# One plan of the order of issue over three stages of an encoder step, in place of three plans

## The chip, the core and the metric

The kernel runs on one core of one Trainium2 chip. The metric is the device time of one execution, in microseconds (us). PE is TensorE (matmul), PEld its weight load, DVE VectorE, ACT ScalarE, POOL GpSimd, and SP the engine whose queue issues every DMA of this kernel.

## The reference, cut to what matters

One layer of a streaming encoder, for a prompt of 2048 rows and a sample of 32 rows that share the weights (width 1024, all float32). Each sub-layer is normalised before and after and added to the residual.

```python
hp = rmsnorm(xp, g_pre_mix)
qa, ka, va, qb, kb, vb, la, r = mix_inputs(hp, w_in, w_alpha2, b_alpha)   # one projection, 3088 columns
oa = chunk_band_prompt(qa, ka, va, rel_bias)         # 8 heads x 64: own 64-row chunk and the 8 before it
ob, sp = gla_recurrence(qb, kb, vb, la, s0, block)   # 4 heads, key 64, value 128, gated, causal
xp = xp + rmsnorm(mix_output(oa, ob, r, g_gla_out, w_o), g_post_mix)

mk, mv = mem_kv(mem_prompt, g_mem, w_mk, w_mv)       # 256 memory rows
xp = xp + rmsnorm(mem_attention(rmsnorm(xp, g_pre_mem), mk, mv, w_mq, w_mo), g_post_mem)   # 4 heads x 256

xp = xp + rmsnorm(swiglu(rmsnorm(xp, g_pre_ffn), w_gate, w_up, w_down), g_post_ffn)        # hidden 2816
# the 32 sample rows go the same way, against cached keys, values and state
```

## The kernel before, in words

Every large product is made from three products of a high and a low part (`split`: ACT rounds a copy, L386, and DVE or POOL subtracts, L390; `mm3` issues the three). `mm3` and some others issue through the helper `led` (L383). The trace shows all these at L383, L386 and L390 whatever calls them, so its rows are told apart by their tiles.

**Stage A** (mixing) takes blocks of 512, 512, 512 and 544 rows. `proj` makes queries, keys, values and gates and puts them in DRAM; `attn` makes band attention (`band_group`: scores `s`, softmax, transposes `pt`, values `po`, L750 and L755) and the gated attention (`gla_mix`: small products `g_s` of 64x64, L922 and L926); `out_proj` makes the output projection (`wops`), a norm (`sqa`), the residual `y` (L1053, L1054; x0r is loaded at L1052 and x1d stored at L1055), a second norm (`sqb`, L1026, L1027, L1033) and the scaled input of stage B (L1061), which is stored in DRAM as `h1d` (L1062). Stage A's last block of `out_proj` comes after all its attention. Stage A also makes the memory's keys and values (`mkd`, `mvd`) and block 0's queries for stage B.

**Stage B** (cross-attention) takes five blocks of 416 rows. `load_kv` loads the memory's keys and values (`kr` L1186, `vr` L1190) and splits them into `kTp` and `vTp`; `mem_h` loads h1d of a block and splits it into `m`; `mem_q` makes queries (`mqps`); `mem_attn` makes scores (`ms`), softmax, transposes (`mpt`) and values (`mpv`, into `mo`); `mem_out` makes the output projection (`mops`) into tiles `y`, and `mem_fin` two norms (`norm_fm`: squares at L402 and L405, sums `n_acc` at L406, a product with ones `n_ps` at L408), the residual (L1304, L1305) and the input of stage C (L1309), stored as `h2d` (L1310). The y tiles of odd blocks (1 and 3) and of even ones lie in different pools. Blocks overlap: while block b's heads run, block b + 1's queries are made, and for the last block the output projection of the one before.

**Stage C** (feed-forward) takes three blocks of 696, 692 and 692 rows, each as two column halves with a Strassen-like scheme of seven products: `ffn_raw` loads h2d into four `hr` tiles (L1367), `ffn_ops` forms seven split operands `mf` from their sums and differences (subtractions at L1352), `unit_w` does the same for weights, `unit` issues products `pg` and `pu`, and `down` the products `pdn`.

Each stage opens pools of on-chip memory of its own and closes them at its end, so a pool of stage B lies over memory that pools of stage A had, and a pool of stage C over pools of stage B and over the weight pool that A and B share. An instruction that first writes such memory waits for the old users; the framework adds these waits.

The order in which each engine issues is planned when the kernel is built. `Order._read` walks the traced instructions and takes each one's duration from a formula (`_cost`), the instructions it must follow (through the tiles that both touch) and the tiles it uses. `_pass` then plays the stage: engines that take the ready instruction with the least due time, tiles that hold one of their tag's buffers from the first use to the last. `queue` makes a first order from the program's own priorities, then three times a backward pass, which gives due times, and a forward pass with them; of the four orders it keeps the one that ends first and writes it down as edges from each instruction to the next of its engine. It was called at the end of each stage, and read only what was traced since the call before:

```python
        traced = self.block.bb.instructions
        at = 0
        if self.last is not None:
            at = next(k for k in reversed(range(len(traced))) if traced[k] is self.last) + 1
        self.last = traced[-1]
        self._read(traced[at:])
```

So each stage's plan began with all engines idle, all its memory free and all its inputs there, and ended where its last instruction did. No edge stood between the chain of one stage and that of the next; how the chains are merged on an engine was left to the framework's scheduler.

Of the kernel before, what the change touches and what calls it, by code (L numbers as in the profile page):

```python
# [17 lines left out]
P = 128  # L18
# [28 lines left out]
class Order:  # L47
# [3 lines left out]

    ENGINES = ("PE", "Activation", "DVE", "Pool", "SP")
    SLOW = 1.1
    PASSES = 3

    def __init__(self, tc):
        self.tc = tc
        self.block = tc.nc.cur_bb  # L60
        self.last = None
        self.edge = mybir.DependencyInfo(mybir.DependencyClass.NoSync, mybir.DependencyReason.DATA)

    @staticmethod
# [6 lines left out]
    def _cost(self, ins, kind, eng, outs, inps):  # L71

        n = self._free(outs[0])
        slow = self.SLOW
        if eng == "PE":
            if any(a.tensor.name.startswith(("ident", "anti")) for a in inps):
                return (max(30.0, n * 0.86) if n < 128 else 110.0), 250.0
            if any(a.dtype == F32 for a in inps):
                if n <= 64 and list(inps[0].ap)[0][1] <= 64:
                    return 45.0, 300.0  # L80
                return 2 * max(n * 0.84, 60.0 if n < 128 else 108.0), 300.0
            t = n * 0.4385 + 6.5
            return (max(t, 111.0 if n >= 128 else 60.0) if n < 256 else t), 250.0
        if eng == "SP":
            return 450.0, 2200.0
        if kind == "InstMemset":
            t = 60 + n * 0.5
        elif eng == "Activation":
            if kind == "InstActivation":
                t = 170 + n * 0.9 + (195 if len(outs) > 1 else 0)  # L90
            else:
                t = 165 + n * (0.87 if outs[0].dtype == F32R else 0.82)
        elif eng == "Pool":
            t = 170 + n * 2.35
        elif kind == "InstTensorCopy":
            t = 150 + n * 1.05
        elif kind == "InstTensorTensor":
            t = 200 + n * 1.15
        elif kind == "InstTensorReduce":
            m = self._free(inps[0])  # L100
            t = 60 + m * (1.95 if m > 2 * n else 1.0)
        elif kind == "InstReciprocal":
            t = 130 + n * 6.4
        elif kind == "InstTensorScalarPtr":
            t = 120 + n * 0.83 if len(inps) < 3 else (230 + n * 1.75 if n > 256 else 200 + n * 1.4)
        else:
            t = 245 + n * 1.05
        return t * slow, 90.0

    @staticmethod  # L110
    def _cells(ap):
# [22 lines left out]
        p0 = ap.offset // row  # L134
        return p0, p0 + pat[0][1], bits

    def _read(self, traced):

        self.ops, self.eng, self.dur, self.lat, self.size, self.prio = [], [], [], [], [], []
        self.pred, self.uses, tile_of = [], [], {}  # L140
        self.tiles = []
        log = []
        for ins in traced:
            kind = type(ins).__name__
            eng = str(ins.engine).split(".")[-1]
            if kind in ("BassTilePoolBoundary", "InstLoadActFuncSet") or eng not in self.ENGINES:
                continue
            outs = [a.bass_ap for a in ins.outs if hasattr(a, "bass_ap")]
            inps = [a.bass_ap for a in ins.ins if hasattr(a, "bass_ap")]
            i = len(self.ops)  # L150
            d, l = self._cost(ins, kind, eng, outs, inps)
            size = 4.0
            for _, c in outs[0].ap:
                size *= c
            pred, use = set(), []
            for aps, wr in ((inps, False), (outs, True)):
                for ap in aps:
                    t = ap.tensor
                    if type(t).__name__ != "Tile":
                        continue  # L160
                    k = tile_of.get(t.name)
                    if k is None:
                        k = tile_of[t.name] = len(self.tiles)
                        self.tiles.append(t)
                        log.append([])
                    if t.space == PSUM:
                        p0, p1, bits, wr_ = 0, P, 1, True
                    else:
                        p0, p1, bits = self._cells(ap)
                        wr_ = wr  # L170
                    keep = []
                    for e in log[k]:
                        j, w, q0, q1, b = e
                        if j != i and (wr_ or w) and q0 < p1 and p0 < q1 and b & bits:
                            pred.add(j)
                        if not (wr_ and j != i and p0 <= q0 and q1 <= p1 and not b & ~bits):
                            keep.append(e)
                    keep.append((i, wr_, p0, p1, bits))
                    log[k] = keep
                    if t.space != DRAM and k not in use:  # L180
                        use.append(k)
            self.ops.append(ins)
            self.eng.append(self.ENGINES.index(eng))
            self.dur.append(d)
            self.lat.append(l)
            self.size.append(size)
            self.prio.append(ins.bass_priority)
            self.pred.append(sorted(pred))
            self.uses.append(use)
        n = len(self.ops)  # L190
        self.succ = [[] for _ in range(n)]
        for i in range(n):
# [14 lines left out]
    def _pass(self, prio, back=None):  # L207
# [21 lines left out]
        parked = {g: [] for g in turn}  # L229
        rest = self.count[:]  # L230
        held = [False] * len(self.tiles)
        ready = [[] for _ in self.ENGINES]
        idle = [True] * len(self.ENGINES)
        start, end = [0.0] * n, [0.0] * n
        events = []
        moved = 0.0
# [78 lines left out]
        return start, end  # L315

    def queue(self):
        traced = self.block.bb.instructions
        at = 0
        if self.last is not None:  # L320
            at = next(k for k in reversed(range(len(traced))) if traced[k] is self.last) + 1
        self.last = traced[-1]
        self._read(traced[at:])
        n = len(self.ops)
        best = None
        prio = self.prio
        for turn in range(self.PASSES + 1):
            start, end = self._pass(prio)
            if best is None or max(end) < best[0]:
                best = (max(end), start)  # L330
            if turn == self.PASSES:
                break
            back, fin = self._pass([-(s + d) for s, d in zip(start, self.dur)], back=end)
            whole = max(fin)
            prio = [whole - b for b in fin]
        start = best[1]
        tail = {}
        for i in sorted(range(n), key=lambda i: (start[i], i)):
            e = self.eng[i]
            if e in tail:  # L340
                self.tc.add_manual_dep(self.ops[i], self.ops[tail[e]].name, self.edge, reason="order of issue")
            tail[e] = i
        return best[0]


@with_exitstack
def encoder_step(ctx, tc, ins, outs):
# [8 lines left out]
    dpool = ctx.enter_context(tc.tile_pool(name="dpool", bufs=1, space=DRAM))  # L356
    RW = dict(reuse_waits="tile")

    order = Order(tc)
    PRI = 4000  # L360
    QLEAD = 0.5
    ident = cpool.tile([P, P], F32, name="ident")
# [793 lines left out]
        o1, o2, fin = out_proj(NB - 1)  # L1156
        merge(o1 + o2 + fin)

    order.queue()


    lo_set[0] = [POOL, DVE]
    dense_lead[0] = 0
    with ExitStack() as ph:
# [150 lines left out]
        for b in range(len(CB)):  # L1315
# [7 lines left out]
            if b != len(CB) - 2:  # L1323
                for it in out:
                    it()

    order.queue()


    wph.close()  # L1330
# [280 lines left out]
                down(gs, us, (0,), dn)  # L1611
                finish_rows(0, xts)

    order.queue()


_INS = ["x_prompt", "x_sample", "mem_prompt", "cache_a_k", "cache_a_v", "state_gla", "cache_mem_k", "cache_mem_v",
# [49 lines left out]
```

## Time and profile before

| | |
|---|---|
| time, median of 3 runs | 3460.98 us (3458.7 to 3461.36) |
| profiled execution | 3458.72 us, its span 3456.9 us |
| mean granted TensorE clock | 0.971 |
| instructions | 60285 |
| DMA | 488.57 MB, mean 141 GB/s |

The span is the time from the first to the last instruction on the core; the time of an execution is a little longer. A stretch such as 1920:1990 is in us from the span's start. An arrow in a row reads "waited for": `[14.49 <-ACT vTp L386]` is 14.49 us of idle time before this instruction that ended when ACT had written vTp. In rows of a line or tile the three numbers are the shortest, the median and the longest duration in ns.

### The profile page before, as it was taken

What the parts mean: (1) busy time and instruction counts of PE and PEld (TensorE: products, weight loads), DVE (VectorE), ACT (ScalarE), POOL (GpSimd) and SP (SyncE); (2) the same over time, 40 slices, a digit from 0 to 9 for tenths busy, and PEclk for the clock granted to TensorE, in tenths of its full rate; (3) what the DMA queues carried; (4) which work ended last, traced back from release to release, by engine and by line L of the source; (5) the groups of instructions that cost most, each with busy time, mean ns of one, the idle gap of its engine ahead of it and who ended that gap; (6) DMA issues with size and microseconds to landing.
All of it is one profiled execution on the core that took longest, in us unless ns stands there. A gap on an engine that the chain in (4) does not pass through costs nothing.

```text
span 3456.9 us, 60285 instructions
## 1 busy us (share of the span) xinstructions
PE 3282.8 (95%) x22211; PEld 3095.9 (90%) x22211; DVE 2395.7 (69%) x4395; ACT 1692.9 (49%) x3730; POOL 1352.5 (39%) x1086
## 2 busy tenths in 40 slices
PE   7999999999999899799999599999899998999998
PEld 6888988999977778799999499999799998899998
DVE  5477777666567887657776776667876667876665
ACT  5455555655455556456655343334443433533334
POOL 3243232132255425434542543334353334543332
PEclk9999999999999999899999699999899999999999
DMA  9765754665356637566653532222242222322223
GB/s 280 247 194 158 231 172 132 192 186 158 114 166 207 207 119 233 170 190 195 186 175 110 191 114 74 74 74 74 87 135 74 74 78 86 104 81 74 74 74 91
DMA packets 550045, 488.57 MB, mean 141 GB/s; under 512 B 48488, under 2 KB 496801, under 8 KB 549749
## 3 DMA queue, kind: packets, MB, share of 16 engines
q1 hardware_dynamic: 549749, 484.71, 46.2%
q8 instruction: 175, 2.87, 0.3%
q14 instruction: 121, 0.99, 0.1%
HBM read 369.68 MB, written 114.91 MB: 140 GB/s over the span
## 4 chain that ended last, share of the span: by engine, by line
PE 49%; DVE 4%; issue 2%; ACT 1%; DMA 1%; POOL 1%; SPq 0%; DVEq 0%; POOLq 0%; ACTq 0%
PE pdn L383 14%; PE pg_X L383 7%; PE pu_X L383 7%; PE mops L383 5%; PE pg_Y L383 3%; PE pu_Y L383 3%; PE mqps L383 2%; PE pg_Z L383 2%; PE pu_Z L383 2%; PE mpv L383 1%; PE ms L383 1%; DVE y L1304 1%; DVE hr L1352 0%; DVE acc L1535 0%; DVE mf L390 0%
## 5 line engine op out<-in xcount | busy, mean ns | idle before, releaser
L383 PE MATMUL pdn<-u,wd 128*128 128x346 f32 (+1 forms) x3168 | 521.9, 323 | 27.8 <-DVE acc L1355 25.5
L383 PEld LDWEIGHTS pdn<-u,wd 128*128 128x128 f32 x3168 | 508.9, 190 | 30.5 <-DVE acc L1355 26.6
L386 ACT CAST wg_s<-wg_r 128x512 fp32r<-128x512 f32 x231 | 139.8, 620 | 405.6 <-DVE wg_r L1352 180.5
L1355 DVE TENSOR_TENSOR acc<-acc,pdn 128x346 f32<-128x346 f32 (+1 forms) x464 | 234.9, 513 | 116.5 <-PE pdn L383 114.4
L390 POOL TENSOR_TENSOR wu_s<-wu_r,wu_s 128x512 fp32r<-128x512 f32 x132 | 192.1, 1465 | 250.9 <-ACT wu_s L386 245.1
L383 PE MATMUL pg_X<-mf,wg_s 128*128 128x346 f32 (+1 forms) x1584 | 282.6, 326 | 1.6 <-DVE mf L390 1.0
L383 PE MATMUL pu_X<-mf,wu_s 128*128 128x346 f32 (+1 forms) x1584 | 276.5, 322 | 0.0
L390 POOL TENSOR_TENSOR wg_s<-wg_r,wg_s 128x512 fp32r<-128x512 f32 x99 | 136.4, 1379 | 329.8 <-ACT wg_s L386 329.8
L383 PEld LDWEIGHTS pg_X<-mf,wg_s 128*128 128x128 f32 x1584 | 259.8, 192 | 3.7 <-ACT mf L386 1.8
L383 PEld LDWEIGHTS pu_X<-mf,wu_s 128*128 128x128 f32 x1584 | 255.7, 189 | 0.3 <-POOL wu_s L390 0.3
L383 PE MATMUL wvr_ps<-wvr_s,mv 128*128 128x256 f32 (+3 forms) x1632 | 225.4, 287 | 0.0
L383 PE MATMUL wops<-om,wo_s 128*128 128x512 f32 (+1 forms) x960 | 206.8, 360 | 2.1 <-DVE y L383 1.3
L383 PEld LDWEIGHTS wvr_ps<-wvr_s,mv 128*128 128x128 f32 (+1 forms) x1632 | 203.6, 183 | 4.3 <-issue 1.5
L383 PE MATMUL mops<-mo,wmo_s 128*128 128x416 f32 x960 | 191.1, 354 | 0.0
L390 POOL TENSOR_TENSOR u<-sg,u 128x346 fp32r<-128x346 f32 (+1 forms) x132 | 141.0, 1078 | 116.6 <-ACT u L386 116.6
L386 ACT CAST wu_s<-wu_r 128x512 fp32r<-128x512 f32 x231 | 134.3, 619 | 101.9 <-DVE wu_r L1352 69.2
L383 PEld LDWEIGHTS mops<-mo,wmo_s 128*128 128x128 f32 x960 | 178.2, 188 | 3.7 <-issue 1.1
L383 PEld LDWEIGHTS wops<-om,wo_s 128*128 128x128 f32 x960 | 152.8, 189 | 26.5 <-issue 2.3
L383 PE MATMUL mqps<-m,wmq_s 128*128 128x416 f32 x768 | 169.2, 363 | 5.2 <-DVE m L390 5.2
L750 PE MATMUL po<-prt,v 128*128 128x128 f32 x1120 | 169.6, 278 | 0.0
L750 PEld LDWEIGHTS po<-prt,v 128*128 128x128 f32 x1120 | 153.0, 193 | 5.3 <-issue 0.6
L383 PE MATMUL pg_Y<-mf,wg_s 128*128 128x346 f32 (+1 forms) x792 | 142.2, 328 | 14.4 <-ACT mf L386 8.3
(410 smaller groups left out, 7942.6 us busy)
## 6 DMA issues: line engine op xcount, KB each, us to landing
wg_r<-in_w_ffn_gate_dram SPq DMA_DIRECT2D x66, 512.0 KB, 4.8
wu_r<-in_w_ffn_up_dram SPq DMA_DIRECT2D x66, 512.0 KB, 3.8
wd_r<-in_w_ffn_down_dram SPq DMA_DIRECT2D x66, 512.0 KB, 3.5
wmq_r<-in_w_mq_dram SPq DMA_DIRECT2D x80, 256.0 KB, 3.1
wmo_r<-in_w_mo_dram SPq DMA_DIRECT2D x80, 256.0 KB, 3.0
wo_r<-in_w_o_dram SPq DMA_DIRECT2D x64, 256.0 KB, 3.2
ks<-kad SPq DMA_DIRECT2D x28, 512.0 KB, 5.5
wvr_r<-in_w_in_dram SPq DMA_DIRECT2D x48, 256.0 KB, 4.0
```

What stands on the lines that cost most here:

```text
L383: return f(*a, **k)
L386: ACT.copy(hi, src)
L390: lo_eng.tensor_tensor(out=lo, in0=src, in1=hi.bitcast(F32), op=ALU.subtract)
L750: PE.matmul(po[:, e * P : e * P + n], lhsT=v[:kk, j, :], rhs=prt[:kk, j, :n], start=j == 0, stop=j == len(rows) - 1)
L1304: DVE.scalar_tensor_tensor(out=y[k], in0=y[k], scalar=gains["g_post_mem"][:, k : k + 1], in1=r, op0=ALU.mult, op1=ALU.mult)
L1355: eng.tensor_tensor(out=out, in0=a, in1=b, op=ALU.add)
```

## The change

`queue` is called once, after stage C, and reads all instructions of the program. `_read` notes where pools are opened and closed. For a pool that lies over memory of closed pools it adds a gate to the plan: a step on no engine, of no duration, that follows every instruction that used those pools, and that every instruction that uses the new pool follows. The three calls at the stages' ends become one. The estimate for a float32 product with up to 64 rows of output per partition and up to 64 partitions of input goes from 45 to 82 ns; in this kernel that is `g_s` and its like. The gates are in the plan alone: they are no instructions, and no waits are added to the program by them.

```diff
     ENGINES = ("PE", "Activation", "DVE", "Pool", "SP")
+    GATE = 5
...
                 if n <= 64 and list(inps[0].ap)[0][1] <= 64:
-                    return 45.0, 300.0
+                    return 82.0, 300.0
...
+        opened, closed, owner = {}, {}, {}
+        for p in self.tc.info.pools:
+            if p.space != DRAM:
+                size = sum(m.bufs * (-(-m.max_size_bytes // P // 32) * 32) for m in dict(p.tag_meta).values())
+                opened[p.alloc_inst.name] = (p.id, p.space, size)
...
+        stack, gone, gate, inside = {}, {}, {}, {}
         for ins in traced:
...
+            if ins.name in opened:
+                p, space, size = opened[ins.name]
+                lo = max([q[2] for q in stack.values() if q[0] == space], default=0)
+                stack[p] = (space, lo, lo + size)
+                before = [q for q, (s, a, b) in gone.items() if s == space and a < lo + size and lo < b]
+                if before:
+                    gate[p] = len(self.ops)
+                    self._add(None, self.GATE, (0.0, 0.0), 0.0, 0, sorted({i for q in before for i in inside.get(q, ())}), [])
+            elif ins.name in closed:
+                space, lo, hi = stack.pop(closed[ins.name])
+                gone = {q: v for q, v in gone.items() if not (v[0] == space and lo <= v[1] and v[2] <= hi)}
+                gone[closed[ins.name]] = (space, lo, hi)
...
                     if t.space != DRAM and k not in use:
                         use.append(k)
+                        p = owner.get(t.name)
+                        inside.setdefault(p, []).append(i)
+                        if p in gate:
+                            pred.add(gate[p])
...
     def queue(self):
-        traced = self.block.bb.instructions
-        at = 0
-        if self.last is not None:
-            at = next(k for k in reversed(range(len(traced))) if traced[k] is self.last) + 1
-        self.last = traced[-1]
-        self._read(traced[at:])
+        self._read(self.block.bb.instructions)
...
             e = self.eng[i]
+            if e == self.GATE:
+                continue
             if e in tail:
                 self.tc.add_manual_dep(self.ops[i], self.ops[tail[e]].name, self.edge, reason="order of issue")
...
-    order.queue()          # at the end of stage A
...
-    order.queue()          # at the end of stage B
...
-    order.queue()          # at the end of stage C
+    issue_order.queue()
```

More of the change, by code (lines that the diff above doesn't have):

```diff
@@ L60, in __init__ @@
         self.block = tc.nc.cur_bb
-        self.last = None
         self.edge = mybir.DependencyInfo(mybir.DependencyClass.NoSync, mybir.DependencyReason.DATA)
@@ L135, in _cells, with _add @@
         return p0, p0 + pat[0][1], bits
+    def _add(self, ins, eng, cost, size, prio, pred, use):
+        self.ops.append(ins)
+        self.eng.append(eng)
+        self.dur.append(cost[0])
+        self.lat.append(cost[1])
+        self.size.append(size)
+        self.prio.append(prio)
+        self.pred.append(pred)
+        self.uses.append(use)
     def _read(self, traced):
@@ L142, in _read @@
         log = []
+        opened, closed, owner = {}, {}, {}
[3 more added lines that the diff above has]
+                opened[p.alloc_inst.name] = (p.id, p.space, size)
+                if p.release_inst is not None:
+                    closed[p.release_inst.name] = p.id
+                for t in p.alloc_inst.bass_pool_tiles or ():
+                    owner[t.name] = p.id
+        stack, gone, gate, inside = {}, {}, {}, {}
         for ins in traced:
@@ L150, in _read @@
             i = len(self.ops)
-            d, l = self._cost(ins, kind, eng, outs, inps)
             size = 4.0
@@ L181, in _read @@
                         use.append(k)
[L182 to L189, printed above, removed]
+                        p = owner.get(t.name)
+                        inside.setdefault(p, []).append(i)
+                        if p in gate:
+                            pred.add(gate[p])
+            self._add(ins, self.ENGINES.index(eng), self._cost(ins, kind, eng, outs, inps), size, ins.bass_priority, sorted(pred), use)
         n = len(self.ops)
@@ L231, in _pass @@
         held = [False] * len(self.tiles)
-        ready = [[] for _ in self.ENGINES]
-        idle = [True] * len(self.ENGINES)
+        ready = [[] for _ in range(self.GATE + 1)]
+        idle = [True] * len(ready)
         start, end = [0.0] * n, [0.0] * n
@@ L342, in queue @@
             tail[e] = i
-        return best[0]
 @with_exitstack
@@ L357, in encoder_step @@
     RW = dict(reuse_waits="tile")
-    order = Order(tc)
+    issue_order = Order(tc)
     PRI = 4000
```

## The prediction

> **What bounds the kernel now.** I read the page first: busy times, then the slices.
>
> ```profile
> span 3456.9 us, 60285 instructions
> PE 3282.8 (95%) x22211; PEld 3095.9 (90%) x22211; DVE 2395.7 (69%) x4395; ACT 1692.9 (49%) x3730; POOL 1352.5 (39%) x1086
> PE   7999999999999899799999599999899998999998
> PEclk9999999999999999899999699999899999999999
> ```
>
> TensorE is the bound: 95% busy. Its row of tenths dips at few places, and at the deepest one, slice 23 of 40, the granted clock falls to 0.6 as well. With so little slack on average, the question is what the dips are worth. The second view is the table of stretches, cut at the dips (columns: length, then busy us and count of PE, PEld, DVE, ACT, POOL, then the granted clock):
>
> ```profile
> 100.00:950.00 850.00, 848.98 (x7036) 776.17 (x7036) 588.42 (x1442) 460.09 (x1130) 237.47 (x216) 1.00 0.59 178
> 1000.00:1400.00 400.00, 374.46 (x2662) 319.44 (x2661) 310.10 (x624) 228.89 (x554) 186.67 (x147) 0.96 0.62 190
> 1430.00:1480.00 50.00, 24.55 (x98) 21.08 (x97) 36.09 (x48) 18.46 (x42) 21.27 (x12) 0.62 0.62 193
> 1600.00:1900.00 300.00, 297.56 (x1724) 284.30 (x1723) 200.62 (x359) 176.11 (x410) 126.55 (x92) 1.00 0.53 161
> 1920.00:1990.00 70.00, 27.62 (x102) 22.18 (x101) 50.98 (x52) 24.11 (x35) 29.12 (x18) 0.59 0.56 181
> 2400.00:2520.00 120.00, 99.80 (x594) 94.83 (x593) 103.72 (x129) 57.45 (x99) 59.19 (x42) 0.91 0.29 90
> 2520.00:2890.00 370.00, 370.00 (x2334) 370.00 (x2333) 246.52 (x388) 145.63 (x286) 151.14 (x120) 1.00 0.29 87
> 2890.00:3000.00 110.00, 91.03 (x537) 87.25 (x536) 92.99 (x115) 53.48 (x91) 49.06 (x34) 0.91 0.29 87
> ```
>
> Inside the stages PE does not stop: idle 1.0 of 850 us in the first half of stage A, 2.4 of 300 in stage B, 0.0 of 370 in stage C. Where stages meet it does. Busy time flatters these stretches, since a matmul at half clock counts double, so I price them by count. Stage B's pace is 1724/300 = 5.75 matmuls per us, so the 98 of 1430:1480 are worth 17.0 us and **33.0 us are lost between A and B**. Stage C's pace is 2334/370 = 6.31, so the 102 of 1920:1990 are worth 16.2 us and **53.8 us are lost between B and C**. The two turns inside stage C, from one block of 692 or 696 rows to the next, lose 120 - 594/6.31 = 25.9 and 110 - 537/6.31 = 24.9 us by the same rule; the end of A (1000:1400) idles 25.5 us. Only the first two, 86.8 us together, are places where one plan ended and another began.
>
> What ends them, first from A to B: PE and the DMA queue in order of time, and the row of the last attention products of A.
>
> ```profile
> 1441.62 1.06 PE L383 MATMUL mqps<-m,wmq_s 128*128 128x416 f32 x2 [5.17 <-DVE m L390]
> 1457.47 2.18 PE L1033 MATMUL sqb_ps<-acc,ones 128*128 128x272 f32 x4 [4.50 <-DVE acc L1027]
> 1474.14 1.06 PE L383 MATMUL mpv<-prR,vTp 128*128 128x416 f32 x2 [14.49 <-ACT vTp L386]
> 1450.36 5.96 SPq L1055 DMA_DIRECT2D x1d<-y  x3
> 1461.76 5.19 SPq L1062 DMA_DIRECT2D h1d<-y  x8
> 1469.11 0.51 SPq L1190 DMA_DIRECT2D vr<-mvd  x1
> L755 DVE COPY o<-po x8: 260/288/295, 1328.2 to 1361.2; 64x128 f32<-64x128 f32 x8
> L383 PE MATMUL mqps<-m,wmq_s 128*128 128x416 f32 x76 | 20.2, 406 | 5.2 <-DVE m L390 5.2
> 1517.14 36.41 PE mops L383 x192
> ```
>
> PE waits 14.5 us for vTp, whose load was issued at 1469, behind A's eleven stores of x1d and h1d, though attention, whose memory vTp takes, had ended at 1361. Meanwhile only 76 of the 192 query products (mqps) of block 1 had been issued (that row is of the stretch 1417:1453); the other 116, which need nothing of A's last chain, are worth 116 x 36.41/192 = 22 us.
>
> From B to C, PE, then SP, ACT and DVE:
>
> ```profile
> 1904.82 19.31 PE L383 MATMUL mops<-mo,wmo_s 128*128 128x416 f32 x101
> 1955.37 1.75 PE L408 MATMUL n_ps<-n_acc,ones 128*128 128x416 f32 x2 [26.95 <-POOL n_acc L406]
> 1971.25 0.66 PE L383 MATMUL pg_Y<-mf,wg_s 128*128 128x348 f32 x1 [8.33 <-ACT mf L386]
> 1924.20 0.37 SPq L1367 DMA_DIRECT2D hr<-h2d  x1
> hr<-h2d SPq DMA_DIRECT2D x2, 696.0 KB, 7.6
> 1956.31 1.35 ACT L386 CAST mf<-hr 128x1392 fp32r<-128x1392 f32 x1 [2.61 <-DMA h2d<-y]
> 1959.83 8.47 DVE L1309 SCALAR_TENSOR_TENSOR y<-y,g_pre_ffn,n_r 128x416 f32<-128x416 f32 x8
> L390 DVE TENSOR_TENSOR mf<-hr,mf x15: 1586/1600/2687, 1957.7 to 2924.3; 128x1384 fp32r<-128x1384 f32 x10, 128x1392 fp32r<-128x1392 f32 x5
> L1352 DVE TENSOR_TENSOR hr<-hr,hr x12: 1586/1602/2687, 1968.2 to 2921.3; 128x1384 f32<-128x1384 f32 x8, 128x1392 f32<-128x1392 f32 x4
> L1309 DVE SCALAR_TENSOR_TENSOR y<-y,g_pre_ffn,n_r 128x416 f32<-128x416 f32 x16 | 14.2, 936 | 1.8 <-ACT n_r L395 1.8
> ```
>
> The last product of B ends at 1924. C's first input (hr) is issued at that moment and lands about 7.6 us later, at 1932. But its first cast, into mf, starts at 1956: it waited for a store of h2d out of block 3's y tiles, whose memory mf takes over. Then DVE runs eight scalings of block 4 (8.47 us) before it goes on with C's operands.
>
> **The change part by part.** No instruction of the computation is added or removed; the planner runs at build time and costs the chip nothing. The three plans (three chains of order edges on each engine, merged by the framework) become one chain on each engine. So the whole effect is which instruction stands behind which, on PE, ACT, DVE, POOL and the SP queue.
>
> *A to B.* One plan sees that vTp's memory is free after attention and that mpv needs it, so the vr loads (4) can stand ahead of the 16 stores of x1d and h1d in SP's queue, and the splits that follow them likewise. The 14.5 us go. What is late next is mo, which lies over A's working tiles and so waits for the sqb chain, to about 1460; under it lie the 22 us of query products. Against a full recovery: DVE is busy 36.1 of the 50 us, most of it A's own residual, and 5.2 + 4.5 us of the waits are for DVE. I keep 14 of the 33.0 us as lost: **-19 us**. Bounds: 0 (DVE keeps the order slow) and -33.
>
> *B to C.* A plan of B alone has no reason to finish block 3's h2 early; now a gate says that C's operand memory hangs on it. With it done under the last 19.3 us and more of mops products, the first cast can start at 1932, the landing, instead of 1956: 24 us. Then seven operands are built by 9 DVE instructions of 1.6 us beside two on POOL: 9 x 1.6 = 14.4 us, and each operand feeds 12 products of gate and 12 of up, 24/6.31 = 3.8 us, more than the 14.4/7 = 2.1 us that DVE takes for one. So PE loses the 8 us to landing, the first split (1.35 + 1.6 = 3 us), about half of the next 13 us, and some 5 us because block 4's h2 (14.2 us of DVE for 16 such scalings in this stretch) must still be done before C's accumulators get their memory: 8 + 3 + 6 + 5 = 22 us lost in place of 53.8. **-32 us**. Bounds: -10 (only the eight scalings move out of the way, 8.47 us and a little) and -43 (11 us stay, landing and first split).
>
> The clock falls to 0.59 in this stretch. [...]
>
> Stores and loads that move in SP's queue: if a load that is ready gets behind a store that is not, everything behind it waits. Both plans have that risk; I cost it at nothing, covered by the weights that lie loaded ahead, and if the cover fails, at about one wait as now seen, 14.5 us.
>
> *The corrected estimate* (45 to 82 ns) is for the 64x64 products of the gated attention:
>
> ```profile
> L926 PE MATMUL g_s<-g_W x1536: 218/218/367, 216.2 to 1285.3; 64*64 64x64 f32 x192
> L926 PE MATMUL g_s<-g_kq x256: 218/218/311, 217.9 to 1285.5; 64*64 64x64 f32 x128
> L922 PE MATMUL g_s<-g_W x128: 218/267/367, 216.2 to 1284.6; 64*64 64x64 f32 x128
> 222.53 0.27 PE L922 MATMUL g_s<-g_W 64*64 64x64 f32 x1
> 223.60 0.33 PE L800 MATMUL pt<-ident,u_sb 128*128 128x128 f32 x1
> ```
>
> The code issues 15 products for each of 4 heads and 16 tiles, 960; the trace has 1920 records, two for one. One head's 30 records (the first and what follows the last are shown) take 223.60 - 222.53 = 1.07 us, 71 ns for a product: 82 is nearer than 45. The plan of A was 960 x 37 ns = 35.5 us short of PE time. What better numbers bring is bounded by A's idle time: 1.0 us in its first half, 25.5 us at its end. I take 0, with -20 and +20 as bounds: a new order there can as well open a gap.
>
> *Stage C.* Its steady part has no idle time and its turns were in one plan before: 0, bounds -5 and +10. If the order puts C's first Silu between B's last Ln and Exp, ScalarE reloads its table, 1.28 us each, on an engine busy 24.11 of 70 us there: hidden.
>
> ```profile
> L1459 ACT ACT_TABLE_LOAD x5 | 6.4, 1283 | 0.1
> ```
>
> The sum: -19 - 32 + 0 + 0 = -51 us against this execution's own 3458.7 (span 3456.9 and 1.8 around it): 3408. The runs' median is 3461.0, 2.3 above it, so **3410**.
>
> **The rivals.**
>
> *The seams stay full of VectorE.* PE's holes close only where order was the cause; DVE is the engine with work in both seams (36.1 of 50 and 51.0 of 70 us), and its work is only rearranged. For: the waits on m, acc and the eight scalings. Against: the 14.5 and 24 us waits were for a load and a store, and DVE has 13.9 and 19.0 us of these stretches idle. Then about 10 us at each seam: 3461 - 20 = 3441.
>
> *Slower: one pass for three stages.* The planner makes four orders and keeps the one with the shortest total; before, each stage kept its own best of four. If the order kept is not A's best, A pays over its whole length, since on an in-order engine one late operand holds everything. Price: were the 850 us that now idle 1.0 to idle as A's end does (25.5 of 400, 6.4%), 54 us more; with the 25.5 us of A's end doubled, 79. It decides from about 51 us on. Then 3461 - 51 + 79 = 3489. For it: nothing in the trace shows how far apart the passes lie. Against: C has no idle time to guard, and A's first half has slack on every engine but PE.
>
> *More than forecast.* Both seams shrink to their bounds (-33, -43) and a third of A's late idle goes (-9): 3376.
>
> *No effect.* The gates are by whole pool, and a coarse gate could bring each seam back to where it is: within 7 us of 3461, 0.2%, about what a measurement of this kernel can tell from no change.
>
> **How the numbers follow.** Forecast 0.55, its own range 3388 to 3436; seams stay full 0.18; slower 0.17; more than forecast 0.05; no effect 0.05. Faster: 0.55 + 0.18 + 0.05 = 0.78; same 0.05; slower 0.17. The range 3376 to 3472 leaves out most of the slower case (0.12), half of the larger gain and a little of the edges, under 0.2.
>
> **What would show it.** Right: the vr loads stand ahead of A's last stores and PE's wait for vTp is gone; the first mf cast follows the landing of hr, not a store of h2d; at the seams PE loses 14 and 22 us by count; the row of tenths shows 8 or more at slice 23 and C's steady part keeps 6.31 matmuls per us. Wrong: idle time inside 100:950, a new wait of PE for DVE's mf or m as long as the old ones, or loads late behind stores in SP's queue.

## The result, and the profile after

| | before | after |
|---|---|---|
| median of the runs timed together (4 and 4) | 3461.17 us | 3429.57 us (3426.61 to 3434.38) |
| profiled execution, its span | 3458.72, 3456.9 us | 3426.61, 3424.8 us |
| mean granted TensorE clock | 0.971 | 0.978 |

The ratio is 0.9911, 95% interval 0.9894 to 0.9928: **31 us faster**, where 51 was forecast. In the code after, most lines stand 25 lower: L383, L386 and L390 are now L408, L411 and L415, L1190 is L1213, L1304 to L1310 are L1327 to L1333, L1352 is L1373.

The page after, with the rows of busy time and the tenths:

```profile
span 3424.8 us, 60285 instructions
PE 3273.3 (96%) x22211; PEld 3090.0 (90%) x22211; DVE 2423.3 (71%) x4395; ACT 1696.1 (50%) x3733; POOL 1354.8 (40%) x1086
PE   7999999999999889999999699998999998899998
PEclk9999999999999989999999899999999999999999
```

Slice 17 of 40 (the seam from A to B) was a 7 at clock 8 and is a 9 at clock 9. Slice 23 (from B to C) was a 5 at clock 6 and is a 6 at clock 8, not the 8 that the prediction named. And slice 15, near the end of A, has become an 8 at clock 8. The same in numbers is the table of stretches after (length, then busy us and count of PE, PEld, DVE, ACT, POOL, then the clock). The seams and turns are cut at the same places of the work, which now come at other times:

```profile
100.00:950.00 850.00, 844.71 (x7028) 772.43 (x7026) 600.31 (x1438) 459.13 (x1130) 237.79 (x216) 1.00 0.59 178
1000.00:1400.00 400.00, 365.03 (x2527) 308.19 (x2527) 309.41 (x621) 228.54 (x555) 187.04 (x147) 0.94 0.62 193
1447.00:1497.00 50.00, 47.08 (x271) 45.53 (x270) 42.18 (x66) 32.01 (x75) 25.54 (x17) 0.97 0.68 217
1905.00:1975.00 70.00, 43.96 (x241) 40.74 (x240) 61.45 (x61) 37.29 (x60) 36.69 (x24) 0.80 0.57 182
2368.00:2488.00 120.00, 99.81 (x594) 94.82 (x593) 103.61 (x132) 57.63 (x100) 60.84 (x42) 0.91 0.30 95
2500.00:2850.00 350.00, 350.00 (x2208) 350.00 (x2207) 230.37 (x364) 137.41 (x269) 139.72 (x110) 1.00 0.26 78
2858.00:2968.00 110.00, 90.97 (x538) 86.86 (x537) 93.40 (x116) 51.10 (x86) 49.38 (x34) 0.91 0.29 86
```

Priced by count, as in the prediction: the 271 products of 1447:1497 are worth 271/5.75 = 47.1 of 50 us, so **3 us are lost from A to B, where 33.0 were**. The 241 of 1905:1975 are worth 241/6.31 = 38.2 of 70 us, so **31.8 us are lost from B to C, where 53.8 were**. Stage C's turns (594 in 120 us, 538 in 110) and its pace (2208/350 = 6.31) are what they were. That makes -30 and -22, 52 us, more than the whole gain, so stretches of 50 and 70 us are not the whole account. Four fixed places of the work, read from the rows below and in the prediction, give an account that adds up: A's last output products, B's last, the first product of C's second operand, and the end. A's last output products (`wops`) end 16.4 us later (1421.6 before, 1438.0 after). From there to B's last `mops` products it is 31.1 us less (502.6, now 471.4). From those to `pg_Y`, the first product of C's second operand, it is 17.5 us less (47.1, now 29.6). From there to the end it is 1485.7 us in both. Together that is -32.1, the difference of the two spans. So the second seam gave 17.5 us and not 22: some of its loss only moved behind the stretch of 70 us (the next 70 us have 426 products, 440 before). And A's end cost 16: PE idles 35.0 us in 1000:1400 where it idled 25.5, and 5.3 us in 100:950 where it idled 1.0.

**A to B.** SP's queue and the rows of `vr` and `vTp`, after:

```profile
1396.06 0.38 SPq L1213 DMA_DIRECT2D vr<-mvd  x1
1405.95 0.37 SPq L1213 DMA_DIRECT2D vr<-mvd  x1
1447.79 0.44 SPq L1080 DMA_DIRECT2D x1d<-y  x1
```
```profile
L411 ACT CAST vTp<-vr x4: 612/618/621, 1403.4 to 1413.1; 128x512 fp32r<-128x512 f32 x4
```

The first and the last of the four loads of `vr` are issued at 1396 to 1406, before the first of the last block's stores (1448), and `vTp` is complete some 65 us before the first `mpv` needs it. What then fills PE while A's residual is made:

```profile
1424.73 13.27 PE L408 MATMUL wops<-om,wo_s 128*128 128x272 f32 x105
1447.22 14.38 PE L408 MATMUL mqps<-m,wmq_s 128*128 128x416 f32 x75
1464.52 0.37 PE L1286 MATMUL mpt<-ident,mpr 104*128 104x104 f32 x2 [2.92 <-DVE mpr L1283]
1480.32 1.30 PE L408 MATMUL mpv<-prR,vTp 128*128 128x416 f32 x6
```

Query products of block 1, in one run of 75 and then in small groups between A's norms (`sqb`) and B's first scores; one wait of 2.9 us is all that is left in this stretch.

**B to C.** The first products of C before (`pg_X`, of its first operand):

```profile
1957.72 0.66 PE L383 MATMUL pg_X<-mf,wg_s 128*128 128x348 f32 x1 [0.59 <-ACT mf L386]
1959.36 3.56 PE L383 MATMUL pg_X<-mf,wg_s 128*128 128x348 f32 x11 [0.99 <-DVE mf L390]
```

PE, ACT and DVE after, from B's last output products on:

```profile
1907.64 1.79 PE L408 MATMUL mops<-mo,wmo_s 128*128 128x416 f32 x7
1930.32 0.66 PE L408 MATMUL pg_X<-mf,wg_s 128*128 128x348 f32 x1 [11.81 <-ACT mf L411]
1935.71 3.56 PE L408 MATMUL pg_X<-mf,wg_s 128*128 128x348 f32 x11 [4.74 <-DVE mf L415]
1939.07 0.49 PE L408 MATMUL pg_Y<-mf,wg_s 128*128 128x348 f32 x1
```
```profile
1919.69 1.35 ACT L411 CAST mf<-hr 128x1392 fp32r<-128x1392 f32 x1
1928.91 1.35 ACT L411 CAST mf<-hr 128x1392 fp32r<-128x1392 f32 x1 [4.74 <-DMA h2d<-y]
```
```profile
1922.27 3.51 DVE L1332 SCALAR_TENSOR_TENSOR y<-y,g_pre_ffn,n_r 128x416 f32<-128x416 f32 x1
1925.71 7.93 DVE L1327 SCALAR_TENSOR_TENSOR y<-y,g_post_mem,n_r 128x416 f32<-128x416 f32 x6
1934.06 1.60 DVE L415 TENSOR_TENSOR mf<-hr,mf 128x1392 fp32r<-128x1392 f32 x1
```

The last `mops` products end at 1909, and C's first product follows at 1930, 21 us later (34 before: 1924 to 1958). The second operand's first product follows them 30 us later (47 before: 1924 to 1971). The first casts of operands, from 1919.7 on, wait for no store. They are of the two operands whose low parts POOL makes. But the cast of the operand that C's first product uses, at 1928.9, still waits for block 3's store of h2d, 4.74 us, and DVE runs six scalings of block 4 (7.93 us) before it makes the low part that the next eleven products need. DVE has 61.45 of 70 us busy, 51.0 before.

**A's end.** PE's groups in 1000:1400, first before, then after (the last column is PE's idle time ahead of the group and what ended it):

```profile
L383 PE MATMUL wops<-om,wo_s 128*128 128x512 f32 (+1 forms) x648 | 149.8, 370 | 2.1 <-DVE y L383 1.3 <-POOL om L390 0.6 <-DVE om L390 0.2
L800 PE MATMUL pt<-ident,u_sb 128*128 128x128 f32 x157 | 29.8, 285 | 1.7 <-DVE u_sb L721 0.9 <-ACT prt L801 0.8
L383 PE MATMUL mvps<-wmv_s,mm 128*128 128x256 f32 x192 | 29.3, 303 | 6.6 <-DVE mvf L1102 6.6
```

```profile
L408 PE MATMUL wops<-om,wo_s 128*128 128x512 f32 (+1 forms) x513 | 137.7, 401 | 7.4 <-ACT om L411 2.7 <-ACT y L408 2.3 <-DVE om L415 1.9
L825 PE MATMUL pt<-ident,u_sb 128*128 128x128 f32 x160 | 30.4, 289 | 7.1 <-DVE u_sb L746 3.6 <-ACT prt L826 3.2
L408 PE MATMUL mvps<-wmv_s,mm 128*128 128x256 f32 x192 | 27.8, 297 | 9.4 <-DVE mvf L1127 7.7 <-POOL wmv_s L415 1.7
```

At 1400 A is 135 output products behind (513 against 648). At 13.27/105 = 0.126 us each that is 17 us, and indeed A's last `wops` products end at 1424.7 + 13.3 = 1438, those of before at 1421.6:

```profile
1418.42 3.15 PE L383 MATMUL wops<-om,wo_s 128*128 128x272 f32 x24
```

The waits are short and spread over three engines' work (softmax parts, gated attention's output, the memory's values): no new wait like those that went, but an order that keeps PE less well fed.

### The profile page after: what moved, and what is told of

Its sections match the earlier page's. It is cut to its first block, busy times and chain, and to the rows that moved or that the text cites. A ratio compares the mean times of both kernels' runs of the same rounds, so it can differ in the third digit from the quotient of the medians.

```text
span 3424.8 us, 60285 instructions
## 1 busy us (share of the span) xinstructions
PE 3273.3 (96%) x22211; PEld 3090.0 (90%) x22211; DVE 2423.3 (71%) x4395; ACT 1696.1 (50%) x3733; POOL 1354.8 (40%) x1086
## 4 chain that ended last, share of the span: by engine, by line
PE 84%; DVE 8%; issue 3%; DMA 2%; ACT 2%; POOL 1%; SPq 0%; DVEq 0%; POOLq 0%; ACTq 0%
PE pdn L408 14%; PE pg_X L408 7%; PE pu_X L408 6%; PE wvr_ps L408 5%; PE wops L408 5%; PE mops L408 4%; PE mqps L408 4%; PE pu_Y L408 3%; PE po L775 3%; PE pg_Y L408 3%; PE wva_ps L408 3%; PE wka_ps L408 3%; PE wqa_ps L408 2%; PE s L408 2%; PE pg_Z L408 2%
## 5 line engine op out<-in xcount | busy, mean ns | idle before, releaser
L408 PE MATMUL pdn<-u,wd 128*128 128x346 f32 (+1 forms) x3168 | 522.0, 323 | 27.8 <-DVE acc L1376 25.5
L408 PEld LDWEIGHTS pdn<-u,wd 128*128 128x128 f32 x3168 | 509.0, 190 | 30.5 <-DVE acc L1376 26.6
L411 ACT CAST wg_s<-wg_r 128x512 fp32r<-128x512 f32 x231 | 139.4, 619 | 402.8 <-DVE wg_r L1373 177.1
L408 PE MATMUL pg_X<-mf,wg_s 128*128 128x346 f32 (+1 forms) x1584 | 282.5, 326 | 21.0 <-ACT mf L411 11.8
L415 POOL TENSOR_TENSOR wu_s<-wu_r,wu_s 128x512 fp32r<-128x512 f32 x132 | 192.6, 1468 | 248.9 <-ACT wu_s L411 241.8
L408 PEld LDWEIGHTS pg_X<-mf,wg_s 128*128 128x128 f32 x1584 | 259.5, 192 | 23.8 <-ACT mf L411 13.1
L408 PE MATMUL pu_X<-mf,wu_s 128*128 128x346 f32 (+1 forms) x1584 | 276.5, 322 | 0.0
L415 POOL TENSOR_TENSOR wg_s<-wg_r,wg_s 128x512 fp32r<-128x512 f32 x99 | 134.3, 1358 | 328.5 <-ACT wg_s L411 326.6
L408 PEld LDWEIGHTS pu_X<-mf,wu_s 128*128 128x128 f32 x1584 | 255.5, 189 | 0.3 <-POOL wu_s L415 0.2
L408 PE MATMUL wops<-om,wo_s 128*128 128x512 f32 (+1 forms) x960 | 211.0, 364 | 7.4 <-ACT om L411 2.7
L408 PE MATMUL wvr_ps<-wvr_s,mv 128*128 128x256 f32 (+3 forms) x1632 | 217.7, 286 | 0.0
L408 PEld LDWEIGHTS wvr_ps<-wvr_s,mv 128*128 128x128 f32 (+1 forms) x1632 | 201.5, 183 | 3.7 <-issue 1.3
L408 PE MATMUL mops<-mo,wmo_s 128*128 128x416 f32 x960 | 195.1, 355 | 1.6 <-DVE wmo_s L415 1.6
L415 POOL TENSOR_TENSOR u<-sg,u 128x346 fp32r<-128x346 f32 (+1 forms) x132 | 142.6, 1090 | 114.9 <-ACT u L411 114.9
L411 ACT CAST wu_s<-wu_r 128x512 fp32r<-128x512 f32 x231 | 134.5, 619 | 99.9 <-DVE wu_r L1373 65.9
L408 PEld LDWEIGHTS mops<-mo,wmo_s 128*128 128x128 f32 x960 | 177.3, 188 | 5.8 <-DVE wmo_s L415 1.9
L408 PEld LDWEIGHTS wops<-om,wo_s 128*128 128x128 f32 x960 | 154.2, 192 | 31.2 <-ACT om L411 2.9
L408 PE MATMUL mqps<-m,wmq_s 128*128 128x416 f32 x768 | 164.7, 358 | 0.0
L408 PEld LDWEIGHTS mqps<-m,wmq_s 128*128 128x128 f32 x768 | 140.5, 190 | 1.7 <-issue 0.3
```

Source lines behind the costliest of these rows:

```text
L408: return f(*a, **k)
L411: ACT.copy(hi, src)
L415: lo_eng.tensor_tensor(out=lo, in0=src, in1=hi.bitcast(F32), op=ALU.subtract)
```

## The experiments

Two questions are open: what each seam's common plan is worth, and what costs A's end, the estimate (82 ns is above the 71 that the trace shows) or the common plan itself (one pass for three stages). Every ratio below is to the kernel before, timed on the same chip, with its 95% interval. The runs are called e1 to e11; positions in a trace are those of one execution.

**The estimate alone, and the plan alone.** The kernel before with the new estimate (e1):

```diff
-                    return 45.0, 300.0
+                    return 82.0, 300.0
```

> Three plans as before, only the estimate of the small products goes from 45 to 82 ns. In the changed kernel stage A's last output projection ends 16 us later than before (1438 against 1421.6). Theory 1, the corrected estimate reorders A's end: A is 16 us longer here too, 3461 + 16 = 3477 us, and PE's idle time in 1000:1400 is about 35 us as after, not 25.5. Theory 2, the common plan does it, because A's end is no longer an end of the plan: A stays as before, 3461 us.

Measured: 3472.12 us, 1.0030 (1.0019 to 1.0042): **10 us slower**, with the three plans as they were, between the two theories and nearer the first. PE's groups in 1000:1400 of this kernel, and its stretch 100:950:

```profile
L383 PE MATMUL wops<-om,wo_s 128*128 128x512 f32 (+1 forms) x539 | 143.0, 399 | 4.9 <-ACT y L383 2.3 <-DVE y L383 1.8 <-POOL om L390 0.6
L800 PE MATMUL pt<-ident,u_sb 128*128 128x128 f32 x160 | 30.3, 285 | 5.9 <-ACT prt L801 4.7 <-DVE u_sb L721 1.2
100.00:950.00 850.00, 842.55 (x6996) 769.50 (x6995) 598.99 (x1433) 458.21 (x1126) 238.24 (x216) 1.00 0.59 177
```

109 output products behind by 1400, and small waits of the same kind as in the kernel after. A's last `wops` products end at 1437.9, where they end after too. So the estimate alone is enough to delay A's end by 16 us, without any common plan. Part of it is lost long before the end: in 100:950 PE idles 7.5 us, where it idled 1.0.

The kernel after with the old estimate (e2):

```diff
-                    return 82.0, 300.0
+                    return 45.0, 300.0
```

> One plan with gates, the estimate left at 45 ns. Theory 1 (the estimate costs 16 us in A): the two seams keep their gains of 31 and 17 us and A its old length, 3461 - 48 = 3413 us. Theory 2 (the common plan costs them): as the changed kernel, 3430 us.

Measured: 3421.09 us, 0.9882 (0.9869 to 0.9896). Its point lies 10 us under the kernel after, and the intervals just touch; with e1 and e6 below the sign is plain. The time lies between the two theories. Its stretch 100:950:

```profile
100.00:950.00 850.00, 848.76 (x7033) 775.85 (x7031) 587.75 (x1441) 460.38 (x1130) 237.14 (x216) 1.00 0.59 178
```

PE idles 1.2 us there, as before the change, so the common plan is not what disturbs A's first part. But its `wops` stand at 563 by 1400, and A's last ones end at 1432.0: even with the old estimate the common plan leaves A 85 products later at 1400, and its end 10 us later, than before. The two delays of A's end don't add up: 16 us by the estimate alone, 10 by the plan alone, 16 by both.

**Which seam gives what.** Both kernels have the gates and the 82 ns; `_read` still tracks all pools but takes only what was traced since the last call, and `queue` is called twice. A alone, then B and C together (e3):

```diff
-    def _read(self, traced):
+    def _read(self, traced, at):
...
-            if kind in ("BassTilePoolBoundary", "InstLoadActFuncSet") or eng not in self.ENGINES:
+            if kind in ("BassTilePoolBoundary", "InstLoadActFuncSet") or eng not in self.ENGINES or place < at:
...
+    issue_order.queue()    # at the end of stage A as well
```

> Two plans, A alone and B with C, the estimate 82 ns. The seam from B to C should be as in the changed kernel (17 us gained), the seam from A to B as before (PE waits some 14 us for vTp, its load behind the stores of h1d). Theory 1 (estimate): A 16 us longer, 3461 + 16 - 17 = 3460 us. Theory 2 (common plan): 3461 - 17 = 3444 us.

Measured: 3452.82 us, 0.9982 (0.9973 to 0.9991), halfway between the two theories. What PE waited for at `mpv` in it (us in all, times, longest), and its stretches at the two seams:

```profile
PE mpv L411 <- ACT vTp L414: 12.6, 1, 12.6
```
```profile
1438.00:1488.00 50.00, 23.58 (x117) 20.35 (x116) 37.78 (x54) 19.64 (x47) 21.57 (x13) 0.69 0.65 202
1925.00:1995.00 70.00, 43.37 (x228) 39.75 (x227) 59.39 (x59) 35.81 (x56) 35.47 (x23) 0.78 0.57 176
```

The old wait for `vTp` is back and the A to B seam has 117 products in 50 us; the B to C seam has 228 in 70 us, near the 241 of the kernel after. The other way round, A and B together and C alone (e4, the same edit, the added call at the end of stage B):

> Two plans, A with B, and C alone, the estimate 82 ns. The seam from A to B should be as in the changed kernel (31 us gained), with A's end 16 us longer under either theory: 3461 + 16 - 31 = 3446 us, and at the seam from B to C the first cast into mf again waits till some 32 us after B's last product. If the gain at B to C does not come from planning B with C, but from B's own new order: 3430 us.

Measured: 3442.13 us, 0.9945 (0.9933 to 0.9958), near the forecast and clear of 3430. Its stretches:

```profile
1449.00:1499.00 50.00, 46.82 (x279) 45.22 (x278) 43.19 (x66) 33.06 (x79) 26.99 (x17) 1.00 0.70 222
1905.00:1975.00 70.00, 31.08 (x136) 26.33 (x135) 55.44 (x58) 28.50 (x45) 29.90 (x19) 0.66 0.63 205
```

279 products in the first seam, 136 in the second. All four kernels have 82 ns, so the four ratios make a square: planning A with B takes 1.0030 to 0.9945 (29 us) or, with B and C already together, 0.9982 to 0.9911 (25 us); planning B with C takes 1.0030 to 0.9982 (17 us) or 0.9945 to 0.9911 (12 us). The seams are nearly additive. The same four places as above, in us, one traced execution of each kernel, show where the gains lie:

| | A's last `wops` end at | from there to B's last `mops` | from there to the first `pg_Y` | from there to the end |
|---|---|---|---|---|
| before (45 ns) | 1421.6 | 502.6 | 47.1 | 1485.7 |
| e1, three plans | 1437.9 | 498.7 | 47.1 | 1487.0 |
| e3, A; B with C | 1429.2 | 500.2 | 32.1 | 1485.6 |
| e4, A with B; C | 1440.7 | 468.0 | 41.0 | 1488.6 |
| after | 1438.0 | 471.4 | 29.6 | 1485.7 |

Planning A with B takes 29 to 31 us out of the second column, and planning B with C 11 to 15 out of the third. Two things go across. In e4, where C is planned alone, the third column is already 6 us shorter than in e1, so about a third of this seam's gain comes without planning C with B. And in e3 A's end comes 8.7 us earlier than in e1, although both plan A alone with 82 ns. What differs there is the gates and what the framework merges behind A, so not all of the 17 us of this side of the square is the seam's.

**What holds the seam from B to C.** One theory: the store of h2d, since `mf`'s first operands take over the memory of block 3's y tiles. The rival: VectorE's work, whatever the memory. In this kernel the operands that are made first lie elsewhere (e5: the kernel after, with the pools of the seven operands opened in another order):

```diff
-        mps = {i: pool(f"cm{i}", 1) for i in (5, 6)}
+        mps = {i: pool(f"cm{i}", 1) for i in (0, 1)}
...
-        mps.update({i: pool(f"cm{i}", 1) for i in (4, 0, 1, 2, 3)})
+        mps.update({i: pool(f"cm{i}", 1) for i in (2, 3, 4, 5, 6)})
```

> The changed kernel (one plan, 82 ns) with the pools of stage C's operands in another order: the first two operands lie over the weight pool, which is free with B's last product, and operands 5 and 6 go to where the others lay, over the y tiles of block 3. If the first product of C waits for block 3's stores of h2d (the first operand's memory), as the trace of the changed kernel says (4.74 us before the cast, cast at 1928.9, the loads landed by about 1920), it starts some 10 us earlier: 3430 - 10 = 3420 us. If VectorE is the limit at this seam (rival), the operands come no earlier than their subtractions and splits allow and the time stays within 3 us of 3430.

Measured: 3429.26 us, 0.9907 (0.9892 to 0.9922), the same as after. PE, ACT and DVE of this kernel:

```profile
1908.49 1.82 PE L408 MATMUL mops<-mo,wmo_s 128*128 128x416 f32 x7
1917.94 0.66 PE L408 MATMUL pg_X<-mf,wg_s 128*128 128x348 f32 x1 [7.64 <-ACT mf L411]
1933.38 3.56 PE L408 MATMUL pg_X<-mf,wg_s 128*128 128x348 f32 x11 [13.26 <-DVE mf L415]
1916.54 1.35 ACT L411 CAST mf<-hr 128x1392 fp32r<-128x1392 f32 x1 [1.20 <-DMA hr<-h2d]
```
```profile
1921.39 1.22 DVE L1327 SCALAR_TENSOR_TENSOR y<-y,g_post_mem,n_r 128x416 f32<-128x416 f32 x2 [1.50 <-ACT n_r L420]
1923.89 7.92 DVE L1327 SCALAR_TENSOR_TENSOR y<-y,g_post_mem,n_r 128x416 f32<-128x416 f32 x6
1931.73 1.60 DVE L415 TENSOR_TENSOR mf<-hr,mf 128x1392 fp32r<-128x1392 f32 x1
1936.14 0.64 DVE L1332 SCALAR_TENSOR_TENSOR y<-y,g_pre_ffn,n_r 128x416 f32<-128x416 f32 x1
```

The wait for the store is gone and C's first product comes 12 us sooner, 8 us after B's last. But it is one product: the next eleven wait 13.26 us for DVE, which runs the same six scalings first. They start at 1933.4, against 1935.7 after. The store was a wait in front of a wait, and the second wait is for VectorE. It is VectorE's order that makes most of it: the cast ends at 1917.9 and the low part takes 1.60 us, yet VectorE first stands idle for 1.50 us before 1921.4, waiting for block 4's `n_r`, then does block 4's work, and makes the low part at 1931.7. No run has an order in which C's low part goes first, so what that would be worth is open.

In the kernel after, DVE's six scalings ran in part while POOL made two of the low parts of `mf` (6.90 us for two). This kernel (e9) gives POOL's two to DVE for stage C's first block:

```diff
-            put(b22, POOL)
+            put(b22, POOL if b else DVE)
...
-            put(b21, POOL)
+            put(b21, POOL if b else DVE)
```

> The changed kernel; for stage C's first block alone the two operands whose low parts POOL makes get them from VectorE. In the changed kernel POOL works 6.90 us on these two just when VectorE does six scalings of block 4 (7.93 us, 1.32 us each, where one took 0.64 us) and a last scaling of block 3 (3.51 us). If VectorE's instructions are longer because POOL works beside them: the six take some 4 us, VectorE gets two splits more of 1.6 us, and PE's second wait at this seam (4.74 us, for a split of mf on VectorE) gets shorter: 3430 - 3 to - 6, about 3425 us. If their length has another cause, VectorE's two splits more come on top: 3430 + 3 = 3433 us.

Measured: 3431.33 us, 0.9921 (0.9907 to 0.9934). Its DVE:

```profile
1933.57 4.26 DVE L1327 SCALAR_TENSOR_TENSOR y<-y,g_post_mem,n_r 128x416 f32<-128x416 f32 x6
1937.75 1.59 DVE L415 TENSOR_TENSOR mf<-hr,mf 128x1392 fp32r<-128x1392 f32 x1
1941.40 1.60 DVE L415 TENSOR_TENSOR mf<-hr,mf 128x1392 fp32r<-128x1392 f32 x1
```

The six scalings take 4.26 us in place of 7.93, but DVE has two more low parts of 1.6 us to make. The wait in front of the eleven products falls from 4.74 to 3.08 us and they start 22.3 us behind B's last product, 26.3 after, as the first theory had it; but the time is no shorter. In the 120 us from the first `pg_Y` on, this execution issues 693 products and the kernel after 719; the difference is worth about 4 us. So neither the memory nor POOL's hold-up shortens the whole by itself. That the amount of VectorE's work is what is left is not shown: in e10 below, without POOL's hold-up, VectorE is busy 20.6 of the 26.5 us from B's last `mops` to the first `pg_Y`, and PE still waits 10.17 us for a low part that stands behind the six scalings.

**What the estimate does.** If 82 hurts because it is above the true 71, then 71 should be best, and 58 worse than 71. In the kernel after (e7; e8 has 58.0 there):

```diff
-                    return 82.0, 300.0
+                    return 71.0, 300.0
```

> The changed kernel with an estimate of 71 ns, what the trace shows for a small product when a head's products run together. Theory 1, an estimate that is too high harms stage A's end, and the true one is best: below both 3421 (45 ns) and 3430 (82 ns), about 3415 us. Theory 2, any other number only reshuffles A's end, by up to 10 us either way: no order between 45, 58, 71 and 82.

> The changed kernel with an estimate of 58 ns. Theory 1: between 45 and 71 ns, about 3418 us. Theory 2: anywhere from 3412 to 3440 us. A third, that a higher estimate costs time in proportion: 3421 + 9 x 13/37 = 3424 us here and 3427 us at 71 ns.

Measured: 71 ns gives 3426.62 us, 0.9901 (0.9886 to 0.9916); 58 ns gives 3416.94 us, 0.9874 (0.9859 to 0.9889). With 45 at 0.9882 and 82 at 0.9911 the points of the small numbers are better than those of the large ones, and the true one is with the large. The theory that blamed the error of 82 against 71 falls: its 3415 us lies outside the interval of 71 ns. The third theory, a cost in proportion, has 71 ns right and its 3424 us for 58 ns outside the interval. That the cost sets in between 58 and 71 is not shown by the times, since the interval of 71 overlaps all three others; 58 against 82 is clear. The traces go the same way: the counts of `wops` in 1000:1400 are 563 (45), 564 (58), 526 (71) and 513 (82). PE's idle time in 100:950 is 1.0 to 1.2 us in the four kernels with 45 ns (before, e2, e6 and e10), 3.4 and 3.9 us in the two with 58 (e8 and e11), and 5.0 to 9.4 us in the seven with 71 or 82, whether with one plan, two or three. This trend with the estimate speaks against the second theory's "no order", at least for A's first part.

**Combinations.** The old estimate with the first operands moved (e6, the edits of e5 and e2 together):

> The same with the old estimate of 45 ns. If the two effects add: 3421 - 10 = 3411 us. If VectorE is the limit: 3421 us.

Measured: 3415.08 us, 0.9871 (0.9855 to 0.9888), the fastest, 46 us under before and 14 under after; against e5, which differs by the estimate alone and whose interval lies clear above (0.9892 to 0.9922), the estimate costs 14 us. The same with the two splits on DVE (e10, the edits of e6 and e9), and the edits of e5 with 58 ns (e11):

> The same with the first operands moved and the estimate at 45 ns, as a version that should beat both kernels. Here the first product of C starts 8 us after B's last, and the next waits 13.26 us for a split on VectorE behind six scalings of 7.92 us. If POOL makes them longer, 3415 - 6 = 3409 us; if not, 3418 us.

> One plan, first operands moved, the estimate at 58 ns. If a lower loss came with 58 ns by its own right, and the moved operands give what they gave at 45 ns (6 us): 3417 - 6 = 3411 us. If numbers of the estimate only reshuffle, anywhere from 3411 to 3430 us.

Measured: 3418.31 us, 0.9883 (0.9870 to 0.9897), and 3416.74 us, 0.9880 (0.9865 to 0.9894). e2, e6, e8, e10 and e11 lie within 6 us of each other, with intervals that overlap: the five lie about 3417 us, and none of these edits is shown to be better than the old estimate alone.

## Why the prediction was right or wrong

The time came 20 us above the forecast, in the range and in the own range of the likeliest case, but of the four terms only stage C's came out at its number. That the sum came so near is partly luck: A to B gave 12 us more than its term, B to C some 14 less, and A's end cost 16 that the sum had at nothing.

- **A to B (-19): mechanism right, mis-sized.** 33.0 lost became 3, not 14; from A's last `wops` to B's last `mops` it is 31 us less, and the square of runs gives 25 to 29 us. The loads went ahead of the stores and the query products lie under A's chain, as the step said. What it kept as lost, for DVE's 36.1 of 50 us, was not needed: DVE is now busy 42.2 of 50 us in the seam, so its idle time there was itself an effect of the order.
- **B to C (-32): mis-sized the other way.** By count 53.8 became 31.8, from B's last `mops` to the first `pg_Y` it is 17.5 us less, and the runs give 12 to 17 us for this seam's plan. The step that failed is "the first cast can start at 1932, the landing", and with it "some 5 us because block 4's h2 must still be done". The first casts did follow the landing, 10 us behind B's last product, but not that of the operand which C's first product uses: it waited 4.74 us more for a store of h2d. And block 4's scalings stand not only before C's accumulators but between that cast and its low part, for 7.93 us. e5 shows that the store by itself did not matter, e9 that POOL's hold-up by itself did not. The rival "the seams stay full of VectorE" fits the busy time in this seam (61.45 of 70 us) and is wrong in the other; but its price was 10 us for each seam, and in e5 VectorE idles 1.50 us while C's low part could be made, so that work and not order holds this seam is not shown.
- **The estimate (0, bounds -20 and +20): wrong by +10** (e1) to +14 us (e5 against e6). The bound held it; the argument that 82 is nearer than 45 and so at worst neutral did not.
- **A's end under the common plan: not in the sum.** e2 has the old estimate, and yet its A is 85 `wops` products late at 1400, 85 x 0.126 = 11 us, and its last `wops` end 10 us later; e6 is 58 late, and 6 us. Part of this is A's last chain giving way to B's products, which the A to B seam gets back; how much is real loss the runs don't separate.
- **The rival "one pass for three stages": not shown.** A did lose, at its end, but three separate plans lose as much with the new estimate (e1). Idle time inside 100:950, a sign that the prediction named for being wrong, did show, 5.3 us where 1.0 was. It goes with the estimate and not with the common plan (7.5 us in e1, 1.2 in e2), and the feared 54 us did not come.
- **Stage C and the table loads: right.** The turns kept their 594 and 537 products (538 after), and from the first `pg_Y` on C takes 1485.7 us in both. The loads went from 15 to 18 in all, on an engine busy 37.3 of 70 us in the seam.

The group of the table loads after that was 5 before (two other lines have 5 each, 4 before, and two have one each in both):

```profile
L1480 ACT ACT_TABLE_LOAD x6 | 7.7, 1283 | 0.1
```

- **SP's queue:** in 1400:2000 PE waits for no load directly. Its only long wait that goes back to DMA at a seam is the store named above, through ACT.
- **The clock:** it rose in the seams with the count of products, 0.59 to 0.80 and 0.62 to 0.97. With 21 us between B's last product and C's first it stays at 0.80 over the 70 us: in that gap (1909.4:1930) it is 0.58, the eleven products from 1935.7 on, at a granted clock of 0.50, took 3.56 us where C's pace gives 11/6.31 = 1.74, and from 1939 to 1945 it is at 0.93. That is about 2 us for products at the lower clock, and the sum has nothing for it. At half the clock these products took twice as long, as the price by count has it; in the kernel before, the eleven `pg_X` products from 1959.4 on took 3.56 us at 0.50 as well.

Not settled: why a nearly true duration for the small products gives A's end a worse order than one that is far too small. That all the waits at A's end are short and on three engines fits a reshuffled greedy order better than one wrong due time, while the trend in 100:950 speaks against mere chance; no run decides it. The gates were not tried by themselves: between e1 and e3, which both plan A alone, A's end moved by 8.7 us, and no run tells whether the gates or the merge with the next plan did it. Nor was an order tried in which VectorE makes C's first low parts ahead of block 4's scalings.

## What to carry to other kernels

Where two separately planned stretches meet, price the hole by the count of products against the pace beside it, and then ask for each hole whether order or work ends it: the engine with idle time inside the hole may be idle because of the order (A to B). A busy engine alone does not answer it either (B to C, 61 of 70 us): there, removing the wait in front only lengthened the next, and what tells work from order is when the awaited instruction's inputs were ready and what its engine did until it issued it. Check the price between fixed places of the work as well, since a loss can move out of the stretch that is counted (22 us by count, 17.5 between places). A planner's cost acts as a dial: try its value by itself, above and below the measured one, before bundling a correction with a change of structure, since here the correction gave back a quarter to a third of the gain. A sum made only of the places that the change aims at misses what a new plan does elsewhere.

## What was not expected of the hardware

VectorE's scalings were longer where GpSimd worked beside them. A scaling of 128x416 takes 0.64 us at its shortest in the kernel after (so too in the row of e5 above, at 1936.14) and 0.71 in the mean of six in e9; in the kernel after, the six took 7.93 us, 1.32 in the mean, and the one issued 0.4 us after POOL began took 3.51. POOL's row at that place:

```profile
1921.86 6.90 POOL L415 TENSOR_TENSOR mf<-hr,mf 128x1392 fp32r<-128x1392 f32 x2
```

POOL's two took 3.48 us (from 1921.86) and 3.47 us (from 1925.29). The first ended at 1925.34, and DVE's scaling of 3.51 us at 1925.78, 0.44 us after it. The six, one by one, go the same way, beside POOL's second and the two operations that follow it:

```profile
1925.29 3.47 POOL L415 TENSOR_TENSOR mf<-hr,mf 128x1392 fp32r<-128x1392 f32 x1
1928.72 1.41 POOL L431 TENSOR_TENSOR n_acc<-n_acc,n_sq 128x416 f32<-128x416 f32 x1
1930.09 1.41 POOL L1328 TENSOR_TENSOR y<-y,xr 128x416 f32<-128x416 f32 x1
```
```profile
1925.71 3.50 DVE L1327 SCALAR_TENSOR_TENSOR y<-y,g_post_mem,n_r 128x416 f32<-128x416 f32 x1
1929.13 1.45 DVE L1327 SCALAR_TENSOR_TENSOR y<-y,g_post_mem,n_r 128x416 f32<-128x416 f32 x1
1930.50 1.45 DVE L1327 SCALAR_TENSOR_TENSOR y<-y,g_post_mem,n_r 128x416 f32<-128x416 f32 x1
1931.87 1.77 DVE L1327 SCALAR_TENSOR_TENSOR y<-y,g_post_mem,n_r 128x416 f32<-128x416 f32 x3
```

Each of the first three began 0.4 us after an operation of POOL and ended 0.45 us after it, whether that one took 3.47 or 1.41 us; the last three, with POOL idle, took 1.77 us together. In e9, where POOL has neither low part to make, the six took 4.26 us. What makes VectorE's operations longer there, no run shows.
